# Three feed-forward layers of a Trainium2 kernel open with two plain f tiles instead of four; two further tiles compute their gate for the first tokens early

## The chip, the cores and the metric

The kernel runs as one program on one core of a Trainium2 chip. The metric is the device time of one execution in microseconds (us). TensorE (PE in the profile) does the matrix products, VectorE (DVE) and ScalarE (ACT) the elementwise work, GpSimd (POOL) a few small steps, and SyncE (SP) issues the DMAs. Matmul results land in eight PSUM banks, which VectorE and ScalarE read.

## The reference

One inference step of a model with two layers (DEPTH = 2), 640 tokens (512 latent, 128 context) of width 1024. Each layer is a half-step feed-forward sub-layer, a token mixer (a Fourier mixer in layer 0, attention in layer 1) and another half-step feed-forward sub-layer. All is fp32.

```
def _swiglu(h, w1, w2):
    gate, up = jnp.split(h @ w1, 2, axis=-1)
    return (jax.nn.silu(gate) * up) @ w2

def _half_ffn(x, m, k, g_pre, g_post, w1, w2):
    h = _modulated_prenorm(x, g_pre, m, k)
    return x + 0.5 * m[:, 3 * k + 2, None] * _rmsnorm(_swiglu(h, w1, w2), g_post)

for i in range(DEPTH):
    x = _half_ffn(x, m, 0, ..., ffn_w1[i, 0], ffn_w2[i, 0])
    x = x + m[:, 5] * _rmsnorm(mixer(_modulated_prenorm(x, ..., 1)), norm_post[i, 1])
    x = _half_ffn(x, m, 2, ..., ffn_w1[i, 1], ffn_w2[i, 1])
```

The six sub-layers are numbered n = 0 to 5. Feed-forward layers are n = 0, 2, 3 and 5; n = 1 is the Fourier mixer, n = 4 the attention. The hidden width of a feed-forward layer is 2816, which is 22 f tiles of 128. Context and latent tokens have their own modulation m.

## The kernel before

**Products.** The 640 tokens are 5 tiles of 128, and for the w1 products two halves of 320 (half 0, half 1). An fp32 operand is split into two fp32r parts, hi on ScalarE (L220) and lo on VectorE (L221). One product of a 128x128 block of weights with a 128x320 block of input is three matmuls, hi·hi, hi·lo, lo·hi (`mm3`, L234 to L236); "a product step" below is such a triple. The splits of weights go through a pool of six pairs `hi`/`lo`; of the f tiles of a plain opening the fourth goes to blocks of the general pool `ring`. Raw weights come by DMA in 512 KB units into four `raw` buffers.

**A plain f tile** (`w1`) has gate and up, two halves and 8 blocks of the model width: 32 product steps, 96 matmuls. ScalarE then takes the silu of the gate (L657), VectorE multiplies by up (L658), and the result is split (`hidden`).

**A fast f tile** (`w1_fast`, L704 to L736) does the same gate and up with seven products of four steps instead of eight: 28 steps, 84 matmuls. It works on sums of weight quarters (VectorE, L195 to L197 and L203) and on differences of input quarters (`combine`, L692). The products land in four PSUM banks: x and y of kind `score`, z in the only bank of kind `turn`, w in the only bank of kind `sum`. Their order is x, y, z, w, then x again, z again (both add to what the bank holds), w2. VectorE joins them: q = y - x (L715), a = q - z (L718), a = a + w (L722), v = q - z (L728), v times silu (L729), -w - q (L733), and the last product (L735). ScalarE copies x (L712) and takes two silus (L725, L734). Nothing of a fast tile can start before both halves of the input are there, since the differences run across the halves.

**A feed-forward layer** follows a plan: plain f 0 and 1 together (`multi`, four banks), f 2, f 3, all on half 0; then the same on half 1 with the four combine steps between; then fast f 4 to 21; slices of w2 are put between the fast tiles; the last slice of w2 ends each token tile in `chain`, which normalizes, adds to the residual, normalizes again for the next layer, waits, and transposes the tile into the next layer's input (L605; ScalarE L614 and VectorE L616 read the two banks and write `y`, which is split again). The transposes of the tiles 2 to 4 therefore lie in the opening of the next layer.

**What sets the order.** All engines' instructions are put in order ahead of time by a scheduler that goes by priorities (`high_priority` steps are put as early as their operands allow) and by explicit "issue after" ties. The time at which a tile's transposes enter the order is set by a counter `now`, which grows by 441.6 per product step of 320 columns; `chain` yields a number by which its transposes are put behind its normalization. `gate_rows` transposes the modulation's gate column of a layer on TensorE into the `turn` bank (L538), ScalarE copies it out (L540), and a DMA spills it. It is called at f = 20: once for the layer itself, and for n = 0 and 3 a second time right after it, for the mixer that follows. Background work (L429, the modulation of layer 1, on VectorE) is put between w2 slices.

Of the kernel before, what the change touches and what calls it, by code (L numbers as in the profile page):

```python
# [24 lines left out]
HALF = TOK // 2  # L25
# [17 lines left out]
FAST = range(4, NF)  # L43
# [83 lines left out]
class Kernel:  # L127
# [54 lines left out]
    def send(self, kind, src):  # L182
# [6 lines left out]
        if kind in ("plain", "block", "gate"):  # L189
            raw = self.raw_tile(src)  # L190
            self.fast["gate"] = raw
        elif kind == "sums":
            up, gate = self.raw_tile(src), self.fast["gate"]
# [370 lines left out]
    def chain(self, n, i, pss, acc=()):  # L564
# [36 lines left out]
        yield {0: 10500, 1: 14000, 2: 9200, 3: 11000, 4: 15000}[i]  # L601
# [19 lines left out]
    def ffn(self, layer, which, base, boundary):  # L621
# [3 lines left out]
        n = layer * 3 + 2 * which  # L625
        begun = [False, False]
# [7 lines left out]
        def w1(fs, half):  # L634
# [8 lines left out]
            elif len(fs) == 1:  # L643
                for f in fs:
                    for j in range(2):
                        with self.behind_of(*[] if n or half else (*self.entered, self.load)):
                            w = self.unit(base + self.w1_at[f] + j)
                        with self.tc.issue_after(self.latest.ins):
                            pss.append(self.proj(w, lambda k: k * P, half, kind="score" if f == 2 and n == 0 else "main"))
            else:  # L650
                pss = self.multi([self.unit(base + self.w1_at[f] + j) for f in fs for j in range(2)], half,
# [46 lines left out]
        def product(f, ps, unit, at, x, start):  # L698
            w = self.unit(base + self.w1_at[f] + unit)
# [4 lines left out]
        def w1_fast(f):  # L704

            g[f] = self.ring(F32R).rearrange("p (a t) -> p a t", a=2)
            a, q = (self.temp("left")[:, :HALF] for _ in range(2))
            s, v = (self.temp("right")[:, :HALF] for _ in range(2))
            x, y, z = (self.bank(kind)[:, :HALF] for kind in ("score", "score", "turn"))
# [3 lines left out]
            product(f, y, 1, 512, lambda k: part(2, k), True)  # L713
            with high():
                tt(q, y, a, op=ALU.subtract)  # L715
            product(f, z, 1, 0, lambda k: part(3, k), True)
# [3 lines left out]
            product(f, w, 2, 0, lambda k: part(1, k), True)  # L720
# [5 lines left out]
            product(f, z, 2, 512, lambda k: part(4, k), False)  # L726
# [4 lines left out]
            product(f, w, 3, 0, lambda k: self.h.chunk(4 + k, 1), False)  # L731
            with high():
                nc.vector.scalar_tensor_tensor(out=q, in0=w, scalar=-1.0, in1=q, op0=ALU.mult, op1=ALU.subtract)  # L733
                nc.scalar.activation(q, q, AF.Silu)  # L734
# [23 lines left out]
        def w2(s, tiles):  # L758
# [7 lines left out]
            for a0, f in [(a, f) for a in range(2) for f in range(f0, f1)] if ends else [(None, f) for f in range(f0, f1)]:  # L766
                w = self.unit(base + self.w2_at[s] + f - f0)
# [20 lines left out]
        for op, a, half in self.ffn_plan:  # L788
# [7 lines left out]
            elif op == "combine":  # L796
                combine(a)
            elif op == "fast":
                w1_fast(a)
# [19 lines left out]
    def plan_ffn(self):  # L819

        plan = []
        for half in (0, 1):
            for i, fs in enumerate(((0, 1), (2,), (3,))):
                plan += [("w1", fs, half)]
                if half:
                    plan += [("combine", step, None) for step in ((), (0, 1), (2, 3))[i]]
        due = 0
        for f in FAST:
            if f == NF - 2:
                plan += [("gates", None, None)]  # L830
            plan += [("fast", f, None)]
# [5 lines left out]
        self.ffn_plan = plan  # L837
        self.ffn_units, self.w1_at, self.w2_at = [], {}, {}
        for op, v, half in plan:
            if op == "fast":  # L840
                self.w1_at[v] = len(self.ffn_units)
                self.ffn_units += [("gate", v, 0), ("sums", v, 1)]
                self.ffn_units += [(kind, None, None) for kind in ("up", "all")]
# [623 lines left out]
```

## Time and profile before

| | us |
|---|---|
| median of 3 runs (2233.34 to 2235.79) | 2234.68 |
| the profiled execution, its time | 2233.16 |
| span of that execution in the profile | 2231.4 |
| TensorE busy in the span | 2198.5 (99%), 13730 matmul records |
| VectorE busy | 1682.5 (75%) |
| ScalarE busy | 1155.6 (52%) |
| GpSimd busy | 43.7 (2%) |

A row of the timeline has the start in us, the duration in us, the engine, the line, the operation, out<-in by the program's names, and the tile; square brackets hold the idle time of the engine before it and what ended it. Rows of a table of waits are: waiting engine, its bank and line, what it waited for; then us in total, times, longest us. Rows of windows are: from and to, length, busy us of PE, PE's weight loads, DVE, ACT, POOL, each with the number of instructions, then the granted TensorE clock, DMA share and GB/s. Rows of groups are: line, engine, operation, out<-in, tile, xcount, then busy us, mean ns of one, then idle us before it with what ended it.

### The profile page before, as it was taken

How to read it: one execution, taken by the hardware profiler on the slowest of the kernel's cores; microseconds unless marked ns; L12 is line 12 of the kernel's file. 1: busy time of each engine (PE TensorE's matmuls, PEld its weight loads, DVE VectorE, ACT ScalarE, POOL GpSimd, SP SyncE). 2: the span in 40 equal slices, each digit the busy share in tenths (PEclk: the TensorE clock that was granted, in tenths of full speed). 3: DMA queues.
4: the chain of work that ended last, by engine and by line, in shares of the span. 5: the costliest groups of instructions: out<-in, count | busy, mean ns of one | idle time of the engine just before them, and what ended most of it. 6: DMA issues, size and time to landing. Idle time of an engine off the chain costs nothing. (4 is left out here: it accounts for less than half of the span.)

```text
span 2231.4 us, 35240 instructions
## 1 busy us (share of the span) xinstructions
PE 2198.5 (99%) x13730; PEld 2051.7 (92%) x13730; DVE 1682.5 (75%) x3081; ACT 1155.6 (52%) x2186; POOL 43.7 (2%) x95
## 2 busy tenths in 40 slices
PE   7999999999999999999999999999999999999998
PEld 5999999999899999998999999989999899999997
DVE  5888898687868898887688898776555666766684
ACT  4544454464544454455444554466878644455452
POOL 0000000010000000001000000000000000000000
PEclk8999999999999999999999999999999999999999
DMA  8144444432413444444144344523343322322232
GB/s 313 67 142 161 140 143 144 178 127 94 167 72 123 139 146 149 154 143 178 57 143 150 133 147 150 195 77 105 108 118 111 106 74 95 114 87 88 101 123 104
DMA packets 84424, 288.13 MB, mean 129 GB/s; under 512 B 9537, under 2 KB 14497, under 8 KB 84129
## 3 DMA queue, kind: packets, MB, share of 16 engines
q1 hardware_dynamic: 83712, 285.23, 37.6%
q8 instruction: 107, 1.75, 0.3%
q10 hardware_dynamic: 544, 0.66, 0.1%
q14 instruction: 61, 0.49, 0.1%
HBM read 270.34 MB, written 11.58 MB: 126 GB/s over the span
## 5 line engine op out<-in xcount | busy, mean ns | idle before, releaser
L220 ACT ACTIVATE hi<-raw 128x1024 fp32r<-128x1024 f32 (+1 forms) x374 | 358.4, 973 | 330.2 <-PE score L235 86.9
L221 DVE TENSOR_TENSOR lo<-raw,hi 128x1024 fp32r<-128x1024 f32 (+1 forms) x374 | 416.0, 1118 | 142.1 <-ACT hi L220 140.9
L234 PE MATMUL main<-hi,ring 128*128 128x512 f32 (+2 forms) x1044 | 391.4, 375 | 0.0
L235 PE MATMUL main<-lo,ring 128*128 128x512 f32 (+2 forms) x1044 | 387.8, 372 | 0.8 <-DVE lo L221 0.8
L236 PE MATMUL main<-hi,ring 128*128 128x512 f32 (+2 forms) x1044 | 387.2, 371 | 0.0
L429 DVE SCALAR_TENSOR_TENSOR junk<-raw,wide 128x1024 bf16<-128x1024 f32 x256 | 313.1, 1223 | 95.7 <-DMA raw<-in_w_mod_t 91.3
L236 PE MATMUL score<-ring,lo 128*128 128x320 f32 x896 | 277.1, 309 | 0.3 <-DVE lo L221 0.3
L234 PE MATMUL score<-ring,hi 128*128 128x320 f32 x896 | 277.4, 310 | 0.0
L235 PE MATMUL score<-ring,hi 128*128 128x320 f32 x896 | 276.9, 309 | 0.0
L234 PEld LDWEIGHTS main<-hi,ring 128*128 128x128 f32 x1044 | 196.3, 188 | 34.9 <-issue 1.7
L235 PEld LDWEIGHTS main<-lo,ring 128*128 128x128 f32 x1044 | 196.3, 188 | 33.8 <-DVE lo L221 1.1
L236 PEld LDWEIGHTS main<-hi,ring 128*128 128x128 f32 x1044 | 196.1, 188 | 33.9 <-issue 0.2
L234 PE MATMUL turn<-ring,hi 128*128 128x320 f32 x648 | 200.5, 309 | 2.3 <-DVE left L718 2.1
L236 PE MATMUL sum<-ring,lo 128*128 128x320 f32 x648 | 200.2, 309 | 0.0
L235 PE MATMUL sum<-ring,hi 128*128 128x320 f32 x648 | 200.2, 309 | 0.0
L234 PE MATMUL sum<-ring,hi 128*128 128x320 f32 x648 | 200.2, 309 | 0.0
L235 PE MATMUL turn<-ring,hi 128*128 128x320 f32 x648 | 200.2, 309 | 0.0
L236 PE MATMUL turn<-ring,lo 128*128 128x320 f32 x648 | 200.2, 309 | 0.0
L781 ACT ACTIVATE y<-main 128x512 f32<-128x512 f32 x160 | 94.2, 591 | 200.0 <-PE main L236 199.0
L234 PE MATMUL main<-ring,hi 128*128 128x320 f32 x560 | 181.8, 325 | 1.6 <-ACT ring L220 1.6
L235 PE MATMUL main<-ring,hi 128*128 128x320 f32 x560 | 174.9, 312 | 0.8 <-DVE ring L221 0.8
L236 PE MATMUL main<-ring,lo 128*128 128x320 f32 x560 | 174.8, 312 | 0.0
(247 smaller groups left out, 4371.4 us busy)
## 6 DMA issues: line engine op xcount, KB each, us to landing
raw<-in_w SPq DMA_DIRECT2D x264, 512.0 KB, 3.9
raw<-in_w_mod_t SPq DMA_DIRECT2D x128, 512.0 KB, 3.5
raw<-in_qkv SPq DMA_DIRECT2D x26, 512.0 KB, 3.8
first<-in_w_mod_k SPq DMA_DIRECT2D x16, 512.0 KB, 8.8
spill<-ring SPq DMA_DIRECT2D x12, 640.0 KB, 2.9
ring<-spill SPq DMA_DIRECT2D x12, 640.0 KB, 7.2
raw<-in_bias SPq DMA_DIRECT2D x16, 448.0 KB, 3.8
raw<-in_four_in SPq DMA_DIRECT2D x8, 512.0 KB, 3.8
```

The lines of the kernel that those rows point to most:

```text
L220: a = self.nc.scalar.activation(hi, src, AF.Copy)
L221: self.last_split = a, self.nc.vector.tensor_tensor(lo, src, hi.bitcast(F32), op=ALU.subtract)
L234: mm(out, whi, xhi, start=start, stop=False)
L235: mm(out, whi, xlo, start=False, stop=False)
L236: self.latest = mm(out, wlo, xhi, start=False, stop=stop)
L429: last = self.nc.vector.scalar_tensor_tensor(out=self.junk, in0=raw, scalar=1.0, in1=self.wide[:, cond, :], op0=ALU.mult, op1=ALU.mult, ac ...
L781: nc.scalar.activation(place(i, a), ps[a], AF.Copy)
```

## The change

For n = 2, 3 and 5 the plan is now: plain f 0 and 1 on half 0; of f 2 and f 3 the gate product alone, on half 0 alone (`first_half`): the lower four blocks of the model width, whose sum ScalarE copies to a block of `ring` as x, then the upper four on top, whose silu goes to the same block; plain f 0 on half 1; the four combine steps; plain f 1 on half 1; then f 2 and f 3 as fast tiles, whose x and silu are already there, so that they compute y, z, w, z again and w2 only (five products); then the fast tiles from 4 on as before. The gate weights of f 2 and f 3 are loaded and split once for the early part ("plain") and the gate is loaded once more for the sums ("again"). Each of the two tiles has 8 + 20 = 28 product steps instead of 32. The layer n = 0 keeps four plain tiles. In `gates`, the second `gate_rows` (for n = 0 and 3) becomes an operation `rows` one f tile later, at f = 21. The chain of tile 4 yields 13000 instead of 15000. The banks x and y are taken once per layer instead of once per tile. A path that would compute the x product of a tile ahead (`open_fast` with `ahead`) is in the code, and `ahead` is None everywhere in the plan.

```
-        yield {0: 10500, 1: 14000, 2: 9200, 3: 11000, 4: 15000}[i]
+        yield {0: 10500, 1: 14000, 2: 9200, 3: 11000, 4: 13000}[i]
...
+        def first_half(fs):
+            room = self.ring(F32).rearrange("p (i t) -> p i t", t=HALF)
+            pss = [self.bank()[:, :HALF] for _ in fs]
+            stash.update({f: (room[:, 2 * i], room[:, 2 * i + 1]) for i, f in enumerate(fs)})
+            for i, f in enumerate(fs):
+                product(f, pss[i], "gate", 0, chunk(0, 0), True)
+                with high():
+                    copy(stash[f][0], pss[i], AF.Copy)
+            for i, f in enumerate(fs):
+                product(f, pss[i], "gate", 512, chunk(4, 0), False)
+                with high():
+                    copy(stash[f][1], pss[i], AF.Silu)
...
-            product(f, x, 0, 0, lambda k: self.h.chunk(k, 0), True)
-            with high():
-                nc.scalar.activation(a, x, AF.Copy)
+            if f in stash:
+                b, s = stash.pop(f)
+            else:
+                open_fast(f)
+                b, s = left(), right()
+                with high():
+                    copy(b, x, AF.Copy)
...
-            product(f, x, 0, 512, lambda k: self.h.chunk(4 + k, 0), False)
-            with high():
-                nc.scalar.activation(s, x, AF.Silu)
+            if f in opened:
+                product(f, x, "gate", 512, chunk(4, 0), False)
+                with high():
+                    copy(s, x, AF.Silu)
...
             elif op == "gates":
                 self.gate_rows(n)
                 self.gates(n)
+            elif op == "rows":
                 if n % 3 == 0:
                     self.gate_rows(n + 1)
...
-    def plan_ffn(self):
+    def plan_ffn(self, n):
+        early = EARLY if n else 4
+        firsts = ((2, 3),) if early == 2 else ((1, 2), (3, 4))
+        last = firsts[-1][-1]
...
+            plan += [("w1", tuple(range(early)), 0)] + [("first", fs, None) for fs in firsts]
+            plan += [("w1", (0,), 1)] + [("combine", step, None) for step in range(4)]
+            plan += [("w1", (f,), 1) for f in range(1, early)]
...
+        for f in range(early, NF):
+            if f >= NF - 2:
+                plan += [(("gates", "rows")[f - NF + 2], None, None)]
```

Lines of the changed kernel stand two or more further down: `mm3` L236 to L238, the split L222 and L223, `gate_rows` L540, the transposes L607 and their reader on VectorE L618, the plain product L661, the joins L755, L759, L763, L770, L771, L775 and L777.

The first place is TensorE at f = 20 and 21 of n = 0, where the gate column is transposed. Bank `sum` is w of one tile, `score` is x of the next. Before:

```order
L234 MATMUL sum_3755<-ring_588,hi_3706 128x320
L235 MATMUL sum_3755<-ring_589,hi_3706 128x320
L236 MATMUL sum_3755<-ring_588,lo_3707 128x320
L538 MATMUL turn_3829<-ident,coef 16x128
L234 MATMUL score_3854<-ring_212,hi_3725 128x320
L235 MATMUL score_3854<-ring_213,hi_3725 128x320
L236 MATMUL score_3854<-ring_212,lo_3726 128x320
L538 MATMUL turn_3843<-ident,coef 16x128
```

Now the second transposition stands 84 product matmuls behind the first, at the start of f = 21:

```order
L236 MATMUL sum_3886<-ring_588,hi_3832 128x320
L237 MATMUL sum_3886<-ring_589,hi_3832 128x320
L238 MATMUL sum_3886<-ring_588,lo_3833 128x320
L540 MATMUL turn_3960<-ident,coef 16x128
L236 MATMUL score_910<-ring_212,hi_3854 128x320
L237 MATMUL score_910<-ring_213,hi_3854 128x320
```

Three product matmuls stood between the two transpositions into the one `turn` bank; now a whole fast tile does.

The second place is VectorE at the first of the new tiles (f = 2) in n = 2. `lo` are lower parts of weights, `sums` sums of weight quarters, `ring_6083` the block with x and the silu. Before, behind the opening, the same f = 2 on half 1 (the last L658 of it) and the first joins of the fast f = 4 read:

```order
L658 TENSOR_TENSOR right_6480<-main_6454,left_6479 128x320
L221 TENSOR_TENSOR ring_6162<-right_6480,ring_6162 128x320
L715 TENSOR_TENSOR left_6503<-score_6507,left_6502 128x320
L718 TENSOR_TENSOR left_6502<-left_6503,turn_6508 128x320
L221 TENSOR_TENSOR lo_6611<-raw_6608,hi_6610 128x1024
L722 TENSOR_TENSOR left_6502<-left_6502,sum_6559 128x320
L195 TENSOR_TENSOR sums_6661<-raw_6647,raw_6659 128x512
L196 TENSOR_TENSOR raw_6659<-raw_6659 128x512
L197 TENSOR_TENSOR sums_6661<-raw_6647,raw_6659 128x512
L221 TENSOR_TENSOR lo_6638<-raw_6635,hi_6637 128x1024
L728 TENSOR_TENSOR right_6505<-left_6503,turn_6508 128x320
```

Now:

```order
L223 TENSOR_TENSOR lo_6317<-sums_6312,hi_6316 128x1024
L755 TENSOR_TENSOR left_6307<-score_6305,ring_6083 128x320
L223 TENSOR_TENSOR ring_5896<-right_6298,ring_5896 128x320
L223 TENSOR_TENSOR lo_6350<-raw_6310,hi_6349 128x1024
L759 TENSOR_TENSOR left_6345<-left_6307,turn_6306 128x320
L223 TENSOR_TENSOR lo_6384<-raw_6308,hi_6383 128x512
L223 TENSOR_TENSOR lo_6410<-raw_6407,hi_6409 128x1024
L763 TENSOR_TENSOR left_6345<-left_6345,sum_6348 128x320
L197 TENSOR_TENSOR sums_6444<-raw_6407,raw_6442 128x512
L770 TENSOR_TENSOR right_6346<-left_6307,turn_6306 128x320
L198 TENSOR_TENSOR raw_6442<-raw_6442 128x512
L771 TENSOR_TENSOR right_6346<-right_6346,ring_6083 128x320
```

Ahead of each of the joins L755, L759, L763 and L770 a split or a sum of weights now stands in the queue.

The third place is VectorE in the opening of n = 3, where tile 3 (first bank of four transposes) and tile 4 of the layer's input are read out of `score`. `right` and `ring_10028` belong to the plain products and the input. Before:

```order
L196 TENSOR_TENSOR raw_10354<-raw_10354 128x512
L600 TENSOR_SCALAR y<-ring_9700,col_10098 128x1024
L197 TENSOR_TENSOR sums_10356<-raw_10316,raw_10354 128x512
L616 TENSOR_SCALAR y<-score_10208,coef 128x2x64 x4
L221 TENSOR_TENSOR ring_10028<-y,ring_10026 128x4x128
L658 TENSOR_TENSOR right_10251<-main_10129,left_10250 128x320
L221 TENSOR_TENSOR ring_10029<-y,ring_10027 128x4x128
L658 TENSOR_TENSOR right_10257<-sum_10131,left_10256 128x320
L221 TENSOR_TENSOR ring_10102<-right_10251,ring_10102 128x320
L221 TENSOR_TENSOR ring_10103<-right_10257,ring_10103 128x320
L616 TENSOR_SCALAR y<-score_10277,coef 128x2x64 x4
```

Now:

```order
L198 TENSOR_TENSOR raw_10107<-raw_10107 128x512
L560 TENSOR_SCALAR col_10081<-col_10079 128x1
L199 TENSOR_TENSOR sums_10109<-raw_10105,raw_10107 128x512
L602 TENSOR_SCALAR y<-ring_9683,col_10081 128x1024
L205 SCALAR_TENSOR_TENSOR raw_10105<-sums_10109,raw_10105 128x512
L618 TENSOR_SCALAR y<-score_10197,coef 128x2x64 x4
L223 TENSOR_TENSOR ring_10011<-y,ring_10009 128x4x128
L223 TENSOR_TENSOR ring_10012<-y,ring_10010 128x4x128
L661 TENSOR_TENSOR right_10262<-main_10118,left_10261 128x320
L618 TENSOR_SCALAR y<-score_10234,coef 128x2x64 x3
```

Six rows stood between the reads of the two tiles' banks (`score_10208` and `score_10277`); now three do (`score_10197` and `score_10234`), and a sum of weights (L205) stands ahead of the first.

More of the change, by code (lines that the diff above doesn't have):

```diff
@@ L42 @@
 SLICES = ((0, 4), (4, 8), (8, 12), (12, 16), (16, 22))
-FAST = range(4, NF)
+EARLY = 2
 BEHIND = (36, 12, 36, 36, 0, 8)
@@ L190, in send @@
             raw = self.raw_tile(src)
-            self.fast["gate"] = raw
-        elif kind == "sums":
-            up, gate = self.raw_tile(src), self.fast["gate"]
+            if kind == "gate":
+                self.fast["next"] = raw
+        elif kind in ("sums", "again"):
+            self.fast["gate"] = self.raw_tile(src[0]) if kind == "again" else self.fast.pop("next")
+            up, gate = self.raw_tile(src[1]), self.fast["gate"]
             raw = self.raw.tile([P, UNIT], F32, tag="raw", name=self.name("sums"))
@@ L650, in w1 @@
             else:
-                pss = self.multi([self.unit(base + self.w1_at[f] + j) for f in fs for j in range(2)], half,
+                pss = self.multi([self.unit(base + w1_at[f, kind]) for f in fs for kind in ("gate", "up")], half,
                                  ("main", "main", "turn", "sum"))
@@ L696, in ffn, with product @@
         high, tt = self.tc.high_priority, nc.vector.tensor_tensor
-        def product(f, ps, unit, at, x, start):
-            w = self.unit(base + self.w1_at[f] + unit)
+        def product(f, ps, kind, at, x, start):
+            w = self.unit(base + w1_at[f, kind])
             for k in range(4):
@@ L702, in product @@
                 self.mm3(ps, w[0][:, a : a + P], w[1][:, a : a + P], *x(k), start and k == 0, k == 3, not start)
-        def w1_fast(f):
-            g[f] = self.ring(F32R).rearrange("p (a t) -> p a t", a=2)
-            a, q = (self.temp("left")[:, :HALF] for _ in range(2))
-            s, v = (self.temp("right")[:, :HALF] for _ in range(2))
-            x, y, z = (self.bank(kind)[:, :HALF] for kind in ("score", "score", "turn"))
-            product(f, x, 0, 0, lambda k: self.h.chunk(k, 0), True)
-            with high():
-                nc.scalar.activation(a, x, AF.Copy)
-            product(f, y, 1, 512, lambda k: part(2, k), True)
-            with high():
-                tt(q, y, a, op=ALU.subtract)
-            product(f, z, 1, 0, lambda k: part(3, k), True)
+        chunk = lambda c, half: lambda k: self.h.chunk(c + k, half)
@@ new lines, in ffn @@
+        parts = lambda i: lambda k: part(i, k)
+        copy = nc.scalar.activation
+        stash, held, opened = {}, {}, []
+        def first_half(fs):
[10 more added lines that the diff above has]
+                    copy(stash[f][1], pss[i], AF.Silu)
@@ new lines, in open_fast, with w1_fast @@
+        def open_fast(f):
+            if f is None or f in opened:
+                return
+            opened.append(f)
+            product(f, held["x"], "gate", 0, chunk(0, 0), True)
+        def w1_fast(f, ahead):
+            g[f] = self.ring(F32R).rearrange("p (a t) -> p a t", a=2)
+            if not held:
+                held.update({kind: self.bank("score")[:, :HALF] for kind in "xy"})
+            x, y = held["x"], held["y"]
+            z = self.bank("turn")[:, :HALF]
+            left, right = (lambda kind=kind: self.temp(kind)[:, :HALF] for kind in ("left", "right"))
+            steps = {
+                "y": lambda: product(f, y, "sums", 512, parts(2), True),
+                "z": lambda: product(f, z, "sums", 0, parts(3), True),
+            }
+            if f in stash:
[5 more added lines that the diff above has]
+                    copy(b, x, AF.Copy)
+            q = left()
+            steps["y"]()
+            with high():
+                tt(q, y, b, op=ALU.subtract)
+            steps["z"]()
+            a, v = left(), right()
@@ L787, in ffn @@
         turn = list(range(TILES))
-        for op, a, half in self.ffn_plan:
+        for op, a, half in plan:
             if op == "w2" and a[0] == end:
@@ L797, in ffn @@
                 combine(a)
+            elif op == "first":
+                first_half(a)
             elif op == "fast":
-                w1_fast(a)
+                w1_fast(a, half)
             elif op == "w2":
```

81 lines of the change are left out of this document (49 added, 32 removed).

## The prediction

> **What bounds the kernel now.** I read the busy times first, then the waits of TensorE, then stretches, then single rows.
>
> ```profile
> PE 2198.5 (99%) x13730; PEld 2051.7 (92%) x13730; DVE 1682.5 (75%) x3081; ACT 1155.6 (52%) x2186; POOL 43.7 (2%) x95
> PEclk8999999999999999999999999999999999999999
> ```
>
> TensorE is busy for 99% of the span, and after the first of the 40 slices its clock is at full. Time can go only where TensorE gets fewer matmuls or waits less. Its waits, by what ended them (us in total, times, longest):
>
> ```profile
> PE turn L331 <- DMA first<-in_w_mod_k: 12.1, 3, 8.9
> PE turn L538 <- ACT rms L540: 2.7, 2, 1.5
> PE turn L234 <- DVE left L718: 2.1, 2, 1.4
> PE main L234 <- ACT ring L220: 1.6, 1, 1.6
> PE score L605 <- ACT ring L220: 0.6, 1, 0.6
> PE main L236 <- DVE ring L221: 0.6, 1, 0.6
> ```
>
> The 12.1 us lie in the start. After it no wait is longer than 1.6 us, and each kind comes once to three times in the whole program. A matmul's own duration is not what it costs, because matmuls overlap. Three successive ones, and a stretch of pure fast tiles:
>
> ```profile
> 622.13 0.31 PE L235 MATMUL main<-ring,hi 128*128 128x320 f32 x1
> 622.27 0.31 PE L236 MATMUL main<-ring,lo 128*128 128x320 f32 x1
> 622.42 0.31 PE L234 MATMUL main<-ring,hi 128*128 128x320 f32 x1
> ...
> 710.90:760.10 49.20, 49.20 (x338) 49.20 (x337) 46.71 (x79) 24.28 (x38) 0.00 (x0) 1.00 0.43 146
> ```
>
> Each shows 0.31 us, but they start 0.15 us apart, and in the stretch 49.20 / 338 = 0.146 us. That is the price of a matmul. The same stretch has VectorE busy for 46.71 of 49.20 us, with TensorE still full: VectorE at 95% need not stop TensorE, if what it does is in the right order. The three openings that change, from the first matmul to the end of the plain tiles:
>
> ```profile
> 613.20:683.70 70.50, 70.50 (x486) 70.48 (x485) 47.72 (x78) 30.27 (x57) 2.13 (x4) 1.00 0.18 65
> 1047.30:1117.80 70.50, 70.50 (x486) 70.44 (x485) 52.19 (x84) 32.78 (x60) 2.45 (x4) 1.00 0.25 87
> 1795.40:1865.80 70.40, 70.40 (x485) 70.38 (x485) 47.72 (x78) 31.48 (x57) 2.13 (x4) 1.00 0.18 65
> ```
>
> TensorE is full in all three; VectorE is free for 22.8, 18.3 and 22.7 us, and the DMA share is a quarter at most.
>
> **Matmuls taken away.** Each of f 2 and f 3 has 28 product steps instead of 32, so 12 matmuls less; two tiles, three layers: 72. At 0.1465 us that is **-10.55 us**. The row supports this as long as TensorE stays the bound.
>
> The Trainium skill's page "TensorE: Matmul & The Clock Gate", section "Back-to-back issue gap", gives N / 2.4 + 2.5 ns for an isolated matmul at full clock, 135.8 ns at 320 columns, and says that in streams of weight load and matmul both set the spacing. By that formula the 72 would be worth an estimated 9.8 us and the result 0.8 us higher; the trace has 146 ns, with a weight load for each matmul, and decides.
>
> **The gate rows.** In n = 0 and 3 a second transposition follows three matmuls behind the first into the same bank, and has to wait until ScalarE has copied the first out:
>
> ```profile
> 400.02 0.27 PE L538 MATMUL turn<-ident,coef 128*16 128x128 f32 x1
> ...
> 401.67 0.25 ACT L540 ACTIVATE rms<-turn 16x128 f32<-16x128 f32 x1
> ...
> 401.97 0.28 PE L538 MATMUL turn<-ident,coef 128*16 128x128 f32 x1 [1.23 <-ACT rms L540]
> ...
> 405.17 0.31 PE L234 MATMUL turn<-ring,hi 128*128 128x320 f32 x1
> ```
>
> The first of the pair shows no wait, and the tile's own next use of the bank (405.17) comes 3.2 us after the second, well over the 1.9 us that the copy took to be done. Moved to f = 21, the second meets what the first meets: the whole 2.7 us (1.23 and 1.5) go, **-2.72 us**. At worst nothing of it goes (0).
>
> **Weights loaded again.** Six more loads of 512 KB, two in each opening. The table of DMA issues has for one (KB each, median us to landing):
>
> ```profile
> raw<-in_w SPq DMA_DIRECT2D x264, 512.0 KB, 3.9
> ```
>
> The DMA is a quarter busy there at most, and the loads are asked for three units ahead: 0, hidden under the products. If the cover failed, a load's landing would stand in the open, at most 3.9 us each.
>
> **VectorE and ScalarE work added.** What the new tiles do, by the groups of before:
>
> ```profile
> L221 DVE TENSOR_TENSOR lo<-raw,hi 128x1024 fp32r<-128x1024 f32 x302 | 367.9, 1221 | 130.3 <-ACT hi L220 129.1
> L221 DVE TENSOR_TENSOR lo<-sums,hi 128x1024 fp32r<-128x1024 f32 x72 | 88.0, 1223 | 7.0 <-ACT hi L220 4.4
> L197 DVE TENSOR_TENSOR sums<-raw,raw 128x512 f32<-128x512 f32 x72 | 49.7, 691 | 2.0
> L221 DVE TENSOR_TENSOR lo<-raw,hi 128x512 fp32r<-128x512 f32 x72 | 49.4, 686 | 11.8 <-ACT hi L220 11.8
> L718 DVE TENSOR_TENSOR left<-left,turn 128x320 f32<-128x320 f32 x72 | 34.9, 484 | 26.1 <-PE turn L236 26.1
> L658 DVE TENSOR_TENSOR right<-main,left 128x320 f32<-128x320 f32 x23 | 11.2, 486 | 16.1 <-PE main L236 14.1 <-ACT left L657 2.0
> L221 DVE TENSOR_TENSOR ring<-right,ring 128x320 fp32r<-128x320 f32 x104 | 50.0, 485 | 5.2 <-ACT ring L220 4.9
> ```
>
> A plain tile: two splits of 1.22, two products and two hidden splits of 0.49, in all 4.4 us. A new tile: four sums of 0.69, three splits of 1.22, one of 0.69, seven joins and two hidden splits of 0.49, in all 11.5 us. So +7.1 per tile, +14.2 per layer, while the stretch gets 3.5 us shorter. Free on VectorE then are 5.1, 0.6 and 5.0 us: full in n = 3, as in the stretch above, but not over. ScalarE gets about 2 us per tile and has half its time free. As throughput: 0.
>
> What counts is order. In an old fast tile x again lies between w and z again, so a join has two products (24 matmuls, 3.52 us) before its bank is written anew. In the new tiles the join of z (L759) and that of w (L763) have one product, 1.76 us. The rows in the section on the change show a split or a sum ahead of each. With one of 1.22 us just begun and the join's own 0.48, 1.70 us are used: it fits, just. Following the order of n = 2 with these durations I get joins that end 0.5 to 1 us after their product: 0 in n = 2 and 3. In n = 5 ScalarE has this in its way:
>
> ```profile
> 1809.69 1.28 ACT L657 ACT_TABLE_LOAD   x1
> 1810.99 0.44 ACT L657 ACTIVATE left<-main 128x320 f32<-128x320 f32 x1
> ```
>
> It puts the first silu 1.28 us back and what follows on VectorE too; I take **+0.3 us** there. Bounds for all twelve joins: 0 each, and the longest wait for L718 seen, 1.4 us each. I stand near the lower end, since of the 72 old tiles two waited.
>
> The page "TensorE: Matmul & The Clock Gate", section "Architectural detail: the array is 16× 32×32, not 1× 128×128", says that the queues of ScalarE and VectorE are strictly first in, first out, and that TensorE can pull forward only weight loads. By that a late join holds every matmul behind it, which speaks against the change; the two waits for L718 agree. What it would come to is the third rival.
>
> **The transposes of tile 4.** A yield of 13000 instead of 15000 at 441.6 per product step is four to five steps, 12 matmuls or 1.76 us, earlier. In n = 3:
>
> ```profile
> 1061.16 1.37 DVE L616 TENSOR_SCALAR y<-score,coef 128x128 f32<-128x128 f32 x4
> ...
> 1063.09 1.03 PE L605 MATMUL score<-ident,y 128*128 128x128 f32 x8
> ```
>
> They come at 1061.33, the first four fill the bank that ScalarE has read, and the second four at 1061.87 want the bank that VectorE reads until 1062.53, or later, since L205 stands ahead now: 0.7 to 1.4, I take **+0.8 us**. In n = 2 and 5 nothing of the kind stands there. From 0 to 1:
>
> ```profile
> 485.56 0.75 DVE L600 TENSOR_SCALAR y<-ring,col 128x1024 f32<-128x1024 f32 x1
> ...
> 486.46 1.07 PE L605 MATMUL score<-ident,y 128*128 128x128 f32 x8 [0.65 <-ACT ring L220]
> ...
> 489.32 0.41 PE L236 MATMUL main<-ring,ring 128*128 128x320 f32 x1 [0.62 <-DVE ring L221]
> ```
>
> The normalized tile (L600) is ready at 486.31, and the transposes already waited. Put five matmuls earlier in the order, they wait 5 x 0.147 = 0.74 longer. The 0.62 at 489.32, a weight split queued behind the tile's work, should go, as that weight is used later now: **+0.12 us**, between -0.6 and +0.8. From 3 to 4 the same step earlier finds its tile ready: 0.
>
> **The second half of the input.** Half 0 of the opening loses the up products of f 2 and f 3 (16 product steps, 48 matmuls, 7.06 us), so half 1 is wanted that much sooner:
>
> ```profile
> 632.62 1.29 DVE L221 TENSOR_TENSOR ring<-y,ring 128x512 fp32r<-128x512 f32 x2
> 643.10 0.31 PE L234 MATMUL main<-ring,hi 128*128 128x320 f32 x1
> ...
> 1067.92 1.29 DVE L221 TENSOR_TENSOR ring<-y,ring 128x512 fp32r<-128x512 f32 x2
> 1077.17 0.31 PE L234 MATMUL main<-ring,hi 128*128 128x320 f32 x1
> ...
> 1816.33 1.29 DVE L221 TENSOR_TENSOR ring<-y,ring 128x512 fp32r<-128x512 f32 x2
> 1825.15 0.31 PE L234 MATMUL main<-ring,hi 128*128 128x320 f32 x1
> ```
>
> The last split of the input is done 9.2, 8.0 and 7.5 us before half 1 starts. Less 7.06, that leaves 2.1, 0.9 and 0.5, and the earlier tile 4 adds up to 1.76: 4.0, 2.7 and 2.3. I take 0.
>
> **The sum.** -10.55 - 2.72 + 0.3 + 0.8 + 0.12 = -12.05 us, from 2233.16 to 2221.1 in the profiled execution. The median of the runs lies 1.52 above that execution, so 2234.68 - 12.05 = **2222.6 us**.
>
> **Rivals.** *Joins late in part.* The twelve joins with one product of room miss it by 0.5 us on the mean: +6.0, 2228.6. For it: a split or a sum ahead of each join can use up 1.70 of the 1.76 us. Against it: only two of the 72 old joins of z made TensorE wait, though with twice the room, and no background work stands among the new tiles.
>
> *The input of half 1 is late.* Two copies and two silus (0.44 us each, as the row of n = 5) and three sums with a split (3.3 us) come into its way, 5.0 us in all, against room of 4.0, 2.7 and 2.3: 1.0 + 2.3 + 2.7 = +6.0, also 2228.6. Against it: most of that work can stand behind the input's splits.
>
> *The other side: VectorE's queue decides.* Each of the twelve joins waits out the longest wait seen for L718, 1.4 us, as splits of 1.22 us stand ahead in rows of two or three: 16.8 us, 2239.4, slower. The gain is eaten at 12.05 / 12 = 1.0 us a join, and the kernel is slower by more than 0.2% from 1.4. For it: the order rows, and n = 3 with 0.6 us of VectorE free. Against: the full stretch at 95%.
>
> *The gate rows still wait* at f = 21, since the bank's reader there is VectorE: 2225.3.
>
> *A matmul is worth its row*, 0.309 us, so 72 give 22.2: 2211.0. Against it: the starts 0.15 apart.
>
> *The clock falls.* The first slice, with its wait of 8.9 us, is the only one with a clock below full. If each opening stopped as long, three times 8.9 less the 12.05 would give 2249, plus slow matmuls behind it. Nothing in the openings stops longer than 1.6. The section "Part 1: The HAM clock gate" of the same page puts the point at about 3.4 us of idle time, after which the clock is half for about as long; an estimate by that is 3.4 + 1.7 us in each opening, 2237.9.
>
> **How the numbers follow.** Chances: forecast 0.64, gate rows 0.03, joins late in part 0.17, half 1 late 0.06, VectorE's queue 0.06, full rows 0.03, clock 0.01. A measurement of this kernel tells about 0.2%, 4.5 us, from no change: faster is under 2230.2, slower over 2239.1. The forecast, the gate rows and the full rows are faster (0.70), so is most of joins late (0.13) and of half 1 late (0.04); their rest (0.06) and a third of VectorE's queue (0.02) is the same: faster 0.87, same 0.08, slower 0.05. The range: below, 2217.5, if tile 4 costs nothing and the 0.62 goes for nothing (1.5 less), n = 5 too (0.3), the two waits for L718 go with the new order (2.1), and the runs lie 1.3 under their median as the fastest did. Above, 2230.5 takes in both cases at 2228.6 with as much again for the runs. Outside are VectorE's queue, the full rows, the clock and edges of the others, 0.2 in all.
>
> **What would show it.** TensorE's matmul records fall by 72. The windows of the three openings with their two new tiles should be 3.5 us shorter, PE full, DVE near 90%. L540 is gone from TensorE's waits. A wait of z again or w2 (`turn` or `sum`, L236) for VectorE's L759 or L763 in f 2 and f 3 would show the joins late; a wait of `main` for a split of `ring` at the start of half 1 the input late; a wait of L607 for L618 at n = 3 the 0.8. Wrong is the prediction if such waits come in all three layers at more than half a us.

## The result and the profile after

| | before | changed |
|---|---|---|
| median of 6 runs each, us | 2234.3 (2232.69 to 2237.09) | 2221.82 (2219.18 to 2223.66) |
| ratio, 95% interval | | 0.9941 (0.9929 to 0.9954) |
| profiled execution, time and span | 2233.16, 2231.4 | 2219.18, 2217.4 |

The change saves 12.5 us of the medians, 10.3 to 15.9 by the interval; forecast were 12.05 and a time of 2222.6. The profiled execution of the changed kernel is the fastest of its six, and lies 14.0 us under that of before. The page's rows of engines and clock, after:

```profile
PE 2187.0 (99%) x13658; PEld 2039.8 (92%) x13658; DVE 1718.2 (77%) x3147; ACT 1168.4 (53%) x2204; POOL 43.7 (2%) x95
PEclk9999999999999999999999999999999999999999
```

13730 - 13658 = 72 matmuls are gone, and TensorE is as full as it was. The three openings, each from the first product of f 0 and 1 to the first matmul of w2, before and then after. (These stretches also hold the fast tile f 4, before as after, which the prediction's words on them left out. Its stretches of 70.50, 70.50 and 70.40 us ended about 0.1 us behind the first matmul of w2.)

```profile
613.19:683.58 70.39, 70.39 (x485) 70.37 (x484) 47.59 (x78) 30.27 (x56) 2.13 (x4) 1.00 0.17 65
1047.25:1117.65 70.40, 70.40 (x486) 70.33 (x484) 52.09 (x84) 32.78 (x59) 2.45 (x4) 1.00 0.25 87
1795.24:1865.63 70.39, 70.39 (x485) 70.37 (x484) 47.55 (x78) 31.58 (x57) 2.13 (x4) 1.00 0.18 65
...
609.53:676.40 66.87, 66.87 (x461) 66.85 (x460) 58.13 (x98) 35.61 (x63) 2.13 (x4) 1.00 0.28 94
1038.45:1105.89 67.44, 67.23 (x462) 66.83 (x460) 63.72 (x106) 37.34 (x65) 2.44 (x4) 1.00 0.31 106
1784.83:1851.77 66.94, 66.94 (x462) 66.85 (x460) 58.15 (x98) 36.77 (x64) 2.13 (x4) 1.00 0.27 92
```

They are 3.52, 2.96 and 3.45 us shorter, 9.93 in all, where 10.55 of matmuls were forecast with 1.1 to be given back. VectorE went from 47.59 to 58.13 us in n = 2, and from 52.09 to 63.72 of 67.44 in n = 3. The gate rows at f = 21 of n = 0, in the timeline:

```profile
410.40 0.31 PE L238 MATMUL sum<-ring,lo 128*128 128x320 f32 x1
410.54 0.27 PE L540 MATMUL turn<-ident,coef 128*16 128x128 f32 x1
```

The transposition starts 0.14 us after the matmul ahead of it and waits for nothing. The 2.7 us of L538 are out of the table of waits, where of the rows that the change touches now stand:

```profile
PE score L607 <- ACT ring L222: 1.2, 1, 1.2
PE score L607 <- DVE y L618: 0.2, 1, 0.2
```

The first new tile, f 2 of n = 2: the joins of z and w on VectorE, the first matmul that writes each bank again, and the stretch of f 2 and f 3 together:

```profile
650.51 0.48 DVE L759 TENSOR_TENSOR left<-left,turn 128x320 f32<-128x320 f32 x1
651.76 0.31 PE L236 MATMUL turn<-ring,hi 128*128 128x320 f32 x1
652.65 0.48 DVE L763 TENSOR_TENSOR left<-left,sum 128x320 f32<-128x320 f32 x1
653.52 0.31 PE L236 MATMUL sum<-ring,hi 128*128 128x320 f32 x1
...
646.48:664.08 17.60, 17.60 (x122) 17.60 (x121) 17.22 (x29) 9.18 (x13) 0.00 (x0) 1.00 0.35 113
```

The join of z ends at 650.99, 0.77 us ahead of need, that of w at 653.13, 0.39 ahead. VectorE is busy for 17.22 of 17.60 us, and TensorE does not notice. In n = 3 and n = 5 the same join of w has less room. Its row and the next matmul into its bank in n = 3, and the stretch of f 2 and f 3 in n = 3:

```profile
1082.38 0.48 DVE L763 TENSOR_TENSOR left<-left,sum 128x320 f32<-128x320 f32 x1
1082.91 0.41 PE L236 MATMUL sum<-ring,hi 128*128 128x320 f32 x1
...
1075.80:1093.57 17.77, 17.77 (x123) 17.60 (x121) 17.43 (x30) 9.32 (x13) 0.00 (x0) 1.00 0.34 111
```

In n = 3 the join ends 0.05 us before that matmul starts, in n = 5 0.09. In n = 3 the matmul is late for it: it starts 0.22 us after the one ahead of it instead of 0.15. The stretch is 0.17 us longer than in n = 2, and 0.06 in n = 5 (17.66), with no idle time in the rows, since the rows of matmuls overlap.

**What differs for another reason.** Two waits of before, 1.43 us at 950.70 and 0.71 at 1231.04 (both L718), are not in the changed kernel's profile, and a new one of 1.73 us stands in the attention, which the change left as it was. Behind each is a load. Rows for the first place and for the attention, of before, then of after:

```profile
941.42 0.33 SPq L172 DMA_DIRECT2D raw<-in_w  x1
947.93 1.06 ACT L220 ACTIVATE hi<-raw 128x1024 fp32r<-128x1024 f32 x1 [5.23 <-DMA raw<-in_w]
950.70 0.41 PE L234 MATMUL turn<-ring,hi 128*128 128x320 f32 x1 [1.43 <-DVE left L718]
```

```profile
934.10 1.37 SPq L172 DMA_DIRECT2D raw<-in_w  x2
939.14 1.06 ACT L222 ACTIVATE hi<-raw 128x1024 fp32r<-128x1024 f32 x1 [3.62 <-DMA raw<-in_w]
...
1538.38 0.90 SPq L172 DMA_DIRECT2D raw<-in_qkv  x2
1544.48 1.06 ACT L222 ACTIVATE hi<-raw 128x1024 fp32r<-128x1024 f32 x1 [3.80 <-DMA raw<-in_qkv]
1548.88 0.45 PE L1307 MATMUL score<-ring,ring 128*128 128x384 f32 x1 [1.73 <-DVE col L1310]
```

From issue to use took 6.5 us before and 5.0 after at the first place. In the attention it took 6.1 us after; before, the same load went out at 1550.88 and was used at 1554.90, 4.0 us, and a second profile of the changed kernel has 3.8. A split of a late weight stands ahead of the join in VectorE's queue, and TensorE waits for the join. So 2.1 us of waits went and 1.7 came, which is one reason why the terms are better counted in the stretches than in the spans, which differ by 14.0.

### The profile page after: what moved, and what is told of

The parts are those of the page before. It is cut to its first block, busy times and chain, and to the rows that moved or that the text cites. A ratio compares the mean times of both kernels' runs of the same rounds, so it can differ in the third digit from the quotient of the medians.

```text
span 2217.4 us, 35215 instructions
## 1 busy us (share of the span) xinstructions
PE 2187.0 (99%) x13658; PEld 2039.8 (92%) x13658; DVE 1718.2 (77%) x3147; ACT 1168.4 (53%) x2204; POOL 43.7 (2%) x95
## 5 line engine op out<-in xcount | busy, mean ns | idle before, releaser
L222 ACT ACTIVATE hi<-raw 128x1024 fp32r<-128x1024 f32 (+1 forms) x386 | 368.8, 968 | 309.7 <-PE score L237 87.8
L223 DVE TENSOR_TENSOR lo<-raw,hi 128x1024 fp32r<-128x1024 f32 (+1 forms) x386 | 427.1, 1113 | 114.6 <-ACT hi L222 113.3
L236 PE MATMUL main<-hi,ring 128*128 128x512 f32 (+2 forms) x1044 | 391.3, 375 | 0.0
L238 PE MATMUL main<-hi,ring 128*128 128x512 f32 (+2 forms) x1044 | 387.3, 371 | 0.0
L236 PE MATMUL score<-ring,hi 128*128 128x320 f32 x920 | 284.9, 310 | 0.0
L238 PE MATMUL score<-ring,lo 128*128 128x320 f32 x920 | 284.4, 309 | 0.4 <-DVE lo L223 0.4
L237 PE MATMUL score<-ring,hi 128*128 128x320 f32 x920 | 284.2, 309 | 0.0
L236 PEld LDWEIGHTS main<-hi,ring 128*128 128x128 f32 x1044 | 196.3, 188 | 34.8 <-issue 1.7
L238 PEld LDWEIGHTS main<-hi,ring 128*128 128x128 f32 x1044 | 196.1, 188 | 34.0 <-issue 0.2
L236 PE MATMUL sum<-ring,hi 128*128 128x320 f32 x672 | 208.1, 310 | 0.4 <-DVE left L763 0.4
L236 PE MATMUL turn<-ring,hi 128*128 128x320 f32 x672 | 208.2, 310 | 0.0
L238 PE MATMUL turn<-ring,lo 128*128 128x320 f32 x672 | 207.7, 309 | 0.0
L237 PE MATMUL turn<-ring,hi 128*128 128x320 f32 x672 | 207.6, 309 | 0.0
L237 PE MATMUL sum<-ring,hi 128*128 128x320 f32 x672 | 207.6, 309 | 0.0
L238 PE MATMUL sum<-ring,lo 128*128 128x320 f32 x672 | 207.6, 309 | 0.0
L236 PE MATMUL main<-ring,hi 128*128 128x320 f32 x560 | 180.9, 323 | 1.6 <-ACT ring L222 1.6
L238 PE MATMUL main<-ring,lo 128*128 128x320 f32 x560 | 174.4, 311 | 0.0
```

What stands on the lines that cost most here:

```text
L222: a = self.nc.scalar.activation(hi, src, AF.Copy)
L223: self.last_split = a, self.nc.vector.tensor_tensor(lo, src, hi.bitcast(F32), op=ALU.subtract)
L236: mm(out, whi, xhi, start=start, stop=False)
L237: mm(out, whi, xlo, start=False, stop=False)
L238: self.latest = mm(out, wlo, xhi, start=False, stop=stop)
```

## The experiments

All ratios are to the kernel before, run on the same chip beside them.

**The gate rows alone.** The kernel before, with this:

```
             elif op == "gates":
                 self.gate_rows(n)
                 self.gates(n)
+            elif op == "rows":
                 if n % 3 == 0:
                     self.gate_rows(n + 1)
...
-            if f == NF - 2:
-                plan += [("gates", None, None)]
+            if f >= NF - 2:
+                plan += [(("gates", "rows")[f - NF + 2], None, None)]
```

> The kernel before with one part of the change alone: the second transposition of a gate column (n = 0 and 3) comes one f tile later. Theory: the two waits of TensorE for the copy out of the turn bank (1.23 and 1.49 us) go and nothing comes in their place, -2.7 us against before (ratio 0.9988), and the row of waits of L538 for L540 is gone from the profile. Rival: the transposition meets VectorE's reading of the same bank at f = 21, and waits of the same size stand there: 0.

Measured: 2230.52 (11 runs) against 2234.23, ratio 0.9983 (0.9974 to 0.9991), -3.7 us, with the forecast 2.7 inside the interval (2.0 to 5.8). No wait for the copy is left, as the theory said; zero is outside the interval, so the rival falls. In its profile, whose order at L718 is that of before, the waits there are smaller too:

```profile
PE turn L234 <- DVE left L718: 0.5, 1, 0.5
```

**The opening alone.** The changed kernel, with this:

```
-        yield {0: 10500, 1: 14000, 2: 9200, 3: 11000, 4: 13000}[i]
+        yield {0: 10500, 1: 14000, 2: 9200, 3: 11000, 4: 15000}[i]
...
                 self.gates(n)
-            elif op == "rows":
                 if n % 3 == 0:
...
-            if f >= NF - 2:
-                plan += [(("gates", "rows")[f - NF + 2], None, None)]
+            if f == NF - 2:
+                plan += [("gates", None, None)]
```

> The changed kernel with the gate rows back to back and the yield of tile 4 back at 15000, so that only the opening with two plain tiles is left. Theory: 72 matmuls at 0.1465 us, -10.5 us, with at most 0.5 of joins against it: about -10.3 against before (ratio 0.9954), 36 us of openings and new tiles 3.5 shorter in each layer, and L540's wait back at about 2.7. Rival 1: the joins of the new tiles are late, and 6 us of it are lost: -4.5 (0.998), with waits of TensorE for L759 or L763 in f 2 and f 3. Rival 2: without the earlier tile 4 the second half of the input is late, waits of main matmuls at the start of half 1.

Measured: 2225.49 (5 runs), ratio 0.9958 (0.9946 to 0.9971), -9.4 us by the ratio (-8.7 by the medians). The openings, and the wait that is back:

```profile
612.07:678.94 66.87, 66.87 (x462) 66.85 (x460) 58.14 (x98) 35.55 (x63) 2.13 (x4) 1.00 0.28 94
1042.12:1109.64 67.52, 67.52 (x461) 66.84 (x460) 63.71 (x106) 37.26 (x65) 2.44 (x4) 1.00 0.31 106
1789.88:1856.76 66.88, 66.88 (x462) 66.85 (x460) 58.18 (x98) 36.89 (x64) 2.13 (x4) 1.00 0.28 95
...
PE turn L540 <- ACT rms L542: 3.0, 2, 1.7
```

3.52, 2.88 and 3.51 us less than before, 9.9 in all: the openings give nearly what the matmuls give, and they give it without the earlier tile 4, whose transposes the second half of the input did not need. Both rivals fall; n = 3 loses about 0.6, in delays of about 0.2 us at three places, two of them the joins of z and w in f 2 (L759 and L763). This profile also has a wait of 2.2 us in the attention, where the changed kernel had 1.7.

**The matmuls put back.** The changed kernel, with this:

```
-            if f in opened:
+            if f not in opened:
+                product(f, x, "sums", 512, chunk(4, 0), True)
+            else:
                 product(f, x, "gate", 512, chunk(4, 0), False)
```

> The changed kernel with the matmuls put back, and nothing else of before: each of the two new tiles in n = 2, 3 and 5 also makes an x product of 12 matmuls, between w and the second z, on weights that are there anyway; nobody reads it. 72 matmuls more, as many as before. Theory: the gain of the openings is the number of matmuls at the pitch of 0.1465 us, so 10.5 us come back: about -2 us against before (ratio 0.999). Rival 1: a matmul costs its row of 0.309 us: 22 us come back, 10 slower than before. Rival 2: the gain came from fewer waits, and the matmuls hide: it stays at -12 (0.9945).

Measured: 2231.07 (11 runs), ratio 0.9984 (0.9976 to 0.9993), -3.6 us. The openings:

```profile
613.25:683.65 70.40, 70.40 (x486) 70.37 (x484) 58.52 (x98) 35.84 (x63) 2.13 (x4) 1.00 0.26 89
1046.45:1117.23 70.78, 70.58 (x486) 70.36 (x484) 64.32 (x106) 37.55 (x65) 2.44 (x4) 1.00 0.31 101
1794.56:1864.96 70.40, 70.40 (x486) 70.37 (x484) 59.15 (x99) 37.05 (x64) 2.13 (x4) 1.00 0.27 92
```

The first and the third are back at the length of before (70.39 and 70.39), and n = 3 is 0.38 us longer, while VectorE does the work of the changed kernel. 10.33 us came back against the changed kernel's stretches for 72 matmuls, 0.143 us each. The rival by whole rows (22 us) and that by waits (0) fall. What is left of the gain, 3.6 us, is the size that the gate rows had alone.

**The joins later.** The changed kernel, with needless subtractions ahead of two joins:

```
             with high():
+                for _ in range(4 * (f not in opened)):
+                    tt(v, q, z, op=ALU.subtract)
                 tt(a, q, z, op=ALU.subtract)
...
             with high():
+                for _ in range(4 * (f not in opened)):
+                    tt(v, q, w, op=ALU.subtract)
                 tt(a, a, w, op=ALU.add)
```

> The changed kernel with VectorE work put in front of the two joins that have one product of room (z and w, in f 2 and f 3 of n = 2, 3 and 5): four needless subtractions of 128x320 each, about 0.4 us apiece from start to start, 1.6 us a join, 24 x 0.4 x 2 = 19 us of VectorE in all. Theory: the joins now end 0.4 to 0.9 us ahead of the need, so about 1.2 us of z and as much of what follows go through: 2 to 3 us a layer, +6 to +9 against the changed kernel, -3 to -6 against before (ratio 0.998), and TensorE waits for the joins at turn and sum in f 2 and f 3. Rival 1: TensorE is not held by them, as VectorE has room in the opening: no change against the changed kernel (0.9945). Rival 2: VectorE sets the end, all 19 us show: 7 slower than before (1.003).

Measured: 2232.05 (11 runs), ratio 0.9989 (0.998 to 0.9998): 10.2 above the changed kernel's median, a little over the 6 to 9 expected, and -2.2 against before. The openings (to the second matmul of w2, as one was put forward):

```profile
612.46:682.12 69.66, 67.89 (x462) 67.04 (x461) 62.97 (x113) 35.66 (x64) 2.13 (x4) 1.00 0.28 94
1048.24:1119.88 71.64, 69.82 (x463) 68.56 (x461) 68.23 (x120) 37.41 (x66) 2.44 (x4) 0.98 0.30 101
1797.19:1867.32 70.13, 68.15 (x463) 67.05 (x462) 62.73 (x112) 36.86 (x65) 2.13 (x4) 1.00 0.27 91
```

They are 2.79, 4.20 and 3.19 us longer than in the changed kernel. Less the 0.23 us of the w2 matmul that each now holds, that is 9.5 in all, nearly the whole loss. Most of it did not come where I had put it. The scheduler answered the later joins with another order on TensorE, products of f 3 ahead of the second z of f 2, and the longest wait of each opening is for weights:

```profile
661.46 0.42 PE L236 MATMUL score<-ring,hi 128*128 128x320 f32 x1 [1.33 <-ACT hi L222]
660.36 1.06 ACT L222 ACTIVATE hi<-sums 128x1024 fp32r<-128x1024 f32 x1 [6.26 <-DVE sums L199]
659.56 0.68 DVE L199 TENSOR_TENSOR sums<-raw,raw 128x512 f32<-128x512 f32 x1
```

TensorE waits for the upper part of a weight sum (1.33 us here, 1.55 in n = 3 and in n = 5), ScalarE for the sum, and the sum stands among the needless subtractions on VectorE. The joins hold TensorE too, that of z (L761) with 0.37 us of idle time in n = 2 and in n = 5, that of w (L767) with less than 0.1 in all three. A delay is longer than the idle time that the rows show for it, since a row lasts 0.31 us where the next could start after 0.15. Counted by the starts of the matmuls, the weight sums cost about 5.2 us and the joins 3.0. The rest, 1.5 us, is in n = 3 alone: 1.4 us after its long wait the granted clock was 0.50 for 3.4 us, and matmuls started 0.27 us apart.

```profile
1099.50:1102.80 3.30, 3.30 (x15) 3.30 (x14) 1.78 (x4) 1.32 (x2) 0.00 (x0) 0.50 0.35 129
```

So 19 us of VectorE cost 10 of the end: neither hidden nor all in the open. The edge is real, and it is close.

**The changed kernel again.** No edit.

> The changed kernel as it is, for a second profile and more runs. Theory: the waits that come from the program's order stand again at the same places and sizes (the transposes of tile 4 from 0 to 1 at 1.2 to 1.7 us, in n = 3 at 0.2; no wait for L542), and -12 against before (ratio 0.9945). The wait of 1.7 us in the attention and those at later fast tiles of n = 3 come from loads that landed late in that one execution: they change place or size. Rival: they come from the order, which the change moved, and stand again as they were.

Measured: 2220.41 (5 runs), ratio 0.9943 (0.993 to 0.9955). The wait in the attention is gone, and the 0.4 us at L763 in a later fast tile of n = 3 are down to 0.1. The openings are 66.87, 67.44 and 66.95 us long, as in the first profile within 0.01. What the order sets stands, the transposes from 0 to 1:

```profile
485.52 1.07 PE L607 MATMUL score<-ident,y 128*128 128x128 f32 x8 [1.63 <-ACT ring L222]
```

Tile 4 of n = 3 again waited 0.21 us. The rival falls.

**The kernel before again.** No edit, one run.

> The kernel before, for a second profile. Theory: the two waits for L718 (1.43 us at 950.7 and 0.71 at 1231.0), which are gone in the changed kernel, come from weights that landed late and differ by over 0.3 us this time; those for L540 (1.23 and 1.49) come from the order and stand within 0.3 us. Rival: all four stand as they were, and the change has removed the two for L718.

Its waits:

```profile
PE turn L234 <- DVE left L718: 4.3, 3, 2.2
PE turn L538 <- ACT rms L540: 2.3, 2, 1.3
```

The two for L718 are 1.91 and 2.25 us now, with a third of 0.18: other sizes at the same places. Those for L540 are 1.34 and 0.96; the second is 0.53 off, more than I had allowed. The places stand in both profiles of before and hardly in those of the changed kernel (none, then 0.1 at the second), but the change has not removed them. The opening alone has 0.92 and 0.49 us there, the matmuls put back 0.57 and 0.84, the joins later 1.29 and 0.66, one plain tile 0.93 and 0.60; the gate rows alone have 0.53 at the first, and the first layer too has neither. The waits go with when a load lands. Counted from the first matmul of f 17 in n = 2 and of f 9 in n = 3, it lands after 7.6 and 6.9 us in the first profile of before and after 8.1 and 8.4 in this one, but after 6.0 and 5.8 in the changed kernel. Both when it leaves (0.7 to 3.1 us after that matmul) and how long it takes (4.6 to 6.5) vary; what makes them vary is open.

**One plain tile.** The changed kernel, with this:

```
-EARLY = 2
+EARLY = 1
```

> The changed kernel with one plain tile in the opening of n = 2, 3 and 5 instead of two, and f 1 to 4 with the gate half done early: 36 matmuls less than the changed kernel, 5.3 us at the pitch. Theory: the cover is gone. Half 1 has only f 0 (7.1 us) before the first new tile wants the differences of the input. In the changed kernel those for z were ready 10.5 us after half 1 began and the last 13.3 us; now z wants its own after 8.8 us, so 1.7 us at the least are waited, and up to 4 since the sums and joins of f 1 now lie among them on VectorE: -1.76 + 1.7 to 4 in each layer, 0 to +7 against the changed kernel, waits of TensorE for the split of the differences. Rival: the differences are made in time by the priorities, and 5.3 us are gained (2216.5, ratio 0.992).

Measured: 2227.84 (11 runs), ratio 0.997 (0.9961 to 0.9978), 6.0 above the changed kernel beside it by the ratios and 7.4 by the medians. The size is at the upper end of the range given (0 to +7), or just over it, and the mechanism is not the one named. The openings and the waits:

```profile
612.97:679.44 66.47, 65.72 (x449) 65.09 (x448) 60.35 (x104) 35.80 (x65) 2.13 (x4) 1.00 0.30 101
1046.13:1114.27 68.14, 66.27 (x449) 65.02 (x448) 65.10 (x111) 36.58 (x66) 2.50 (x4) 1.00 0.33 111
1796.15:1862.61 66.46, 65.71 (x450) 65.09 (x448) 61.23 (x105) 36.91 (x66) 2.12 (x4) 1.00 0.30 103
...
PE score L236 <- ACT hi L222: 4.1, 2, 2.1
PE score L238 <- DVE lo L223: 3.7, 10, 0.4
```

Two of the three are still 0.4 and 0.5 us shorter than in the changed kernel, though 1.76 was taken away, and n = 3 is 0.7 longer. Nobody waits for the differences of the input. The lower parts of weights come 0.37 us late in the new tiles, and 4.1 us are lost behind the openings, at 723 and 1158, where the next loads leave later among the background's. Behind the second of these, 1.97 us long, the granted clock was 0.50 from 1159.2 to 1162.6. The second bank of tile 4 in n = 3 waited 0.75 us (L618), where it was 0.2. Splits of weights give out first, not the differences.

**The first layer too.** The changed kernel, with this:

```
-        early = EARLY if n else 4
+        early = EARLY
```

> The changed kernel with the opening of n = 0 changed as the others: 24 matmuls less, 3.5 us at the pitch. Theory: VectorE is too full there. It is busy for 47.8 of the 60 us from 40 to 100; with 14.2 more in 56.5 it lacks 5.5 us, part of which later tiles give back: 0 to +5 against the changed kernel, with waits of TensorE for VectorE between 40 and 120, and at the start the loads, which take the DMA for 0.96 to 0.98 of the time until 40. Rival: VectorE's work is put off behind the opening as in n = 3, and the 3.5 us are gained (2218.5).

Measured: 2225.89 (5 runs), ratio 0.9965 (0.9951 to 0.9979), 4.9 above the changed kernel by the ratios, within what the theory gave; the rival falls. Two waits that now have their second and larger part in n = 0, and TensorE from 62 us on:

```profile
PE main L236 <- ACT ring L222: 3.4, 2, 1.8
PE main L237 <- DVE ring L223: 1.9, 2, 1.1
...
62.00:64.00 2.00, 0.32 (x3) 0.06 (x1) 2.00 (x3) 2.00 (x5) 0.00 (x0) 1.00 0.15 33
64.00:66.00 2.00, 0.73 (x2) 0.51 (x3) 2.00 (x4) 1.97 (x5) 0.00 (x0) 0.90 0.65 229
66.00:68.00 2.00, 2.00 (x9) 2.00 (x9) 2.00 (x5) 1.06 (x3) 0.00 (x0) 0.50 0.00 0
68.00:70.00 2.00, 2.00 (x11) 1.92 (x11) 2.00 (x4) 1.15 (x2) 0.00 (x0) 0.75 0.00 0
```

Half 1 finds its input not split: on VectorE two splits of weights (1.22 us each) stand ahead of it, and both ScalarE and VectorE are full (2.00 of 2.00). TensorE is idle for nearly 3 of 4 us, and then the granted clock is 0.50. This is the rival "the clock falls" of the prediction, in a place where there is no room. It is not the only loss of this profile. At 152 and 154 TensorE waits for weights again, 0.43 and 1.13 us, and the clock is at 0.50 from 154.4 to 157.8. Before all that, at 36, it waits 4.39 us for a load, where the changed kernel's two profiles have 1.90; whether the new opening does this or chance, one profile cannot tell.

## Why the prediction was right, and where it was off

- **Matmuls taken away, -10.55.** Right in mechanism and size: in n = 2, where nothing is lost, 24 matmuls less make 3.52 us, 0.147 each. The openings alone are 9.9 us shorter, losses included, and putting 72 matmuls back brings 10.33 us. A matmul's 0.309 us row was rightly not used.
- **Gate rows, -2.72.** Right: nothing waits in their place, and alone they measure -3.7 (-2.0 to -5.8). The term is a little small, since idle time in the rows counts only from the end of the row ahead: from the transposition at f = 20 of n = 0 to the first product of n = 1 the profiles of before and after differ by 1.4 us, and f 17 to 21 of n = 3 take 63.46 us before and 61.83 with the gate rows alone, 1.6. That makes 3.0, and 2.6 from the second profile of before.
- **Weights loaded again, 0.** No wait in the new openings is for DMA.
- **Joins, 0 in n = 2 and 3, +0.3 in n = 5.** The place was partly wrong. The joins cost 0.17 us in n = 3, where 0 was forecast, and at most 0.06 in n = 5. I had worked out that they end 0.5 to 1 us after their product. They end 0.7 to 1.3 after it for z and 0.9 to 1.7 for w, and at 1.6 the room is used up: the "it fits, just" of the prediction came true in f 2 of n = 3 and n = 5. The table load of n = 5 is not what does it, as the join of w in n = 3 is as late (1.61 against 1.65 us) without one. With tile 4 at 15000 n = 3 loses 0.65 against n = 2, and n = 5 nothing.
- **VectorE, +14.2 us a layer, as throughput 0.** The work was counted too high: over the whole run VectorE is busy for 35.7 us more, 11.9 a layer. Part of the reason is that its rows overlap as the matmuls' do: L755 of f 2 in n = 3 lasts 0.48 us, and the next row starts 0.40 after it did. In n = 3, where 0.6 us were to be free, 3.7 were.
- **Tile 4, +0.8 in n = 3 and +0.12 from 0 to 1.** The second bank made TensorE idle for 0.21 us. By the starts it cost 0.4, not 0.8: the eight transposes and what follows take 1.18 us there and 0.79 in n = 2. In the changed kernel VectorE reads tile 3's bank sooner than I had followed. From 0 to 1 the wait grew from 0.65 to 1.18 (1.63 in the second profile), 0.5 to 1.0 for a forecast 0.74, and the one of 0.62 is gone, as forecast.
- **Half 1 of the input, 0.** Right: no wait at its start, with or without the earlier tile 4.
- **The sum.** -12.05 for -12.5 measured. By stretches it is -9.93 for the openings, -2.6 to -3.0 for the gate rows and -0.4 to +0.1 for 0 to 1 (the first stretch of products of n = 1, 85.89 us before, 85.53 and 85.98 after), in all -12.4 to -13.3. The terms were off by 0.2 to 0.4 us each, in both directions, so that the sum is nearer than its parts. In the profiled execution's 14.0 the late loads that went (2.1 us) and came (1.7) nearly cancel, and 1.9 us were gone before any of the changed places: the first gate row of n = 0 came at 398.1, 400.0 before, and at 398.7 to 402.3 in other profiles of kernels with the same opening of n = 0.
- **The rivals.** Half 1 late and gate rows still waiting did not come, and joins late in part came with 0.2 us instead of 6.0. VectorE's queue decides only once two joins get 1.6 us of other work each, and even then the kernel stays a little under before. The clock did not fall in the changed kernel's openings, but what the prediction set against that, that nothing there stops longer than 1.6 us, was no safeguard: in the joins later it fell behind a wait of 1.55.

The 135.8 ns of "Back-to-back issue gap" in "TensorE: Matmul & The Clock Gate" (the Trainium skill) would give an estimated 9.8 us for 72 matmuls. The matmuls put back show 10.33, 0.143 each, nearer to the trace's 0.1465 than to the formula.

## What to carry to other kernels

When one engine is full, price a removed instruction by its pitch in a full stretch, and put as many useless ones back to see whether that was the gain. Then look at what the new order leaves to the engines that serve it: here the step from four plain tiles to two fits with 0.4 us to spare in n = 2 and less than 0.1 in n = 3 and n = 5, and one tile less, or the same step in a layer whose VectorE has less room, costs more than it saves. Count terms in stretches between fixed points of the program, which repeat to 0.1 us, and not in whole runs, which differ by 4 us; the profiles show late loads, and a fallen clock behind some of them, as what differs. And look for waits among overlapping rows by the starts: a matmul 0.2 us late leaves no idle time behind.

## What the hardware showed

- The same load of 512 KB took 6.1 us from issue to use in one execution of the changed kernel and 3.8 in another; the first put a wait of 1.7 us into TensorE.
- After TensorE had been idle for nearly 3 of 4 us (62 to 66, the first layer too), the granted clock was 0.50 from about 65.6 to 69.0 us: 0.4 us at half clock by the mean of 0.90, 2.0, and 1.0 by the mean of 0.75, 3.4 us in all, and matmuls started 0.27 us apart. The Trainium skill, "TensorE: Matmul & The Clock Gate", Part 1 ("The HAM clock gate"), gives about 3.4 us for one such window; the trace agrees on its length, though no single idle stretch here was 3.4 us long (the longest was 1.81).
- A shorter wait can be enough. Between start and end, the ten profiles have six such falls, each 3.4 us long: behind one wait of 1.55 us (the joins later), of 1.91 and of 2.25 (the kernel before again), of 1.97 (one plain tile), and behind two close together (1.81 and 1.14, 0.43 and 1.13, the first layer too). Other waits of this size had none behind them: 1.43 (before), 1.73 (changed), 2.10 (one plain tile), 2.24 (the opening alone), and in the joins later the same 1.55 in n = 5. A fall costs about 1.5 us, an estimate from some 13 matmuls that start 0.27 instead of 0.15 us apart.
